# mLSTM chunks between the projection pairs, and two heads in turns in a recurrence's tile

## The chip, the cores and the metric

The program runs on one core of a Trainium2 chip. Its time is the device time of one launch, in microseconds (us). The kernel before takes 2728.09 us, the median of 3 runs (2724.17 to 2729.37).

A core has five engines that run their own instruction lists in order and wait for each other by semaphores: TensorE (PE, matmuls; PEld is its weight loads), VectorE (DVE), ScalarE (ACT), GpSimd (POOL) and SyncE (SP), which here issues all DMA transfers. Matmuls write to PSUM, which has eight banks; everything else lies in SBUF or in device memory.

## What is computed

One decoder layer of width 1024 on 2048 tokens in float32, and a final norm. The normalised input goes through one wide projection (`w_in`, 1024 to 10256 columns). Its columns feed four branches of width 512, and 4 x 1024 gates:

```python
h = rmsnorm(x, norm_g)
u = h @ w_in                         # split into the inputs of the branches and "merge"
y_a = rg_lru(causal_conv(lru_x)) * silu(lru_z)
hm  = mlstm_chunkwise(q, k, v, log_i, log_f)      # 4 heads of 128
y_b = (head_layernorm(sigmoid(m_o) * hm) + m_skip * xm) * silu(m_z)
y_c = head_rmsnorm(gla_chunkwise(hq, hk, h_i, log_fh)) * silu(h_z)     # 4 heads, key width 128
y_d = head_rmsnorm(gla_chunkwise(g_q, g_k, g_v, log_gk)) * silu(g_z)   # 4 heads, key width 64
merged = sum_n sigmoid(merge_n) * (y_n @ w_branch_n)
out = rmsnorm(x + merged @ w_out, final_g)
```

The mLSTM carries a 128 x 129 state per head from chunk to chunk, with stabilised exponentials. `gla_chunkwise` is a gated linear recurrence: within a chunk a lower triangular matrix of decayed query-key products times the values, plus the query times the carried state.

## The kernel before, in words

The 2048 tokens are done in two halves of 1024, and each half runs through the same stages. A float32 projection is split in two parts (`hi` and `lo`, rounded by ScalarE and subtracted by GpSimd) and done in three matmuls.

1. *Pairs* (`ahead_pairs`, 50 to 740 us in the first half, 1405 to 2085 us in the second). `ip_pair` projects two 128-column tiles for all 1024 tokens with seven products of twelve matmuls (L423), a block scheme that trades an eighth product for additions on VectorE (L428 on weights, L432 on results). The table `GORD` lists which pairs come in which order: `g` for the gates of the merge, `z` for the inputs of the branches, which are kept in device memory, `r` for the RG-LRU (done at once, with its matmuls L743), `d` for a decay, `m` for a step of the mLSTM's gate rows (`mlstm_rows`, L787 and L826), `t` for the change to the exponential and logarithm tables. Products go to the eight PSUM banks in turn (`bank8`).
2. *Mixers* (`mixers`, 740 to 1185 us and 2085 to 2545 us). Twelve tiles of the recurrences (`gla_tile`, 512 tokens each): eight of one head with key width 128 (HGRN2), then four of two heads with key width 64 (GLA), whose keys lie in partitions 0 to 63 and 64 to 127. A tile builds the triangular matrix from the diagonal outwards (L993, then L1036 for the blocks off the diagonal), transposes the keys (L1058), adds to the state (L1064), and forms the outputs: L1079 (matrix times values) and L1080 (query times state), which add up in one bank per head. Between the tiles the values are projected (`ip_vals`, L280) and some gates (L268). The mLSTM (`mlstm`, eight chunks of 128 tokens per half) runs beside them as a second generator: `both` advances it by 0.65 steps (`RATE`) for each step of a tile, after a start of eight steps (`LEAD`). Its matmuls are L863, L872, L879, L888, L900, L908, L909, L919 and L941, four or eight at a time.
3. *Merge* (`merge`): 32 products of a branch with `w_branch` (L268), each multiplied by its gate; its first products run already beside the last tiles of the mixers. Then the output projection (`outp`, L280).

The instructions are written in this order with priorities (`prio`), and a list scheduler places them: each engine's list is fixed when the program is built, by the durations that the scheduler assumes. On the chip an engine does not leave that order. TensorE's list therefore has, between the matmuls of a recurrence, a number of projection matmuls that was chosen to cover the wait.

Temporary tiles come from an arena of 16 slots (`NU`, of 516 columns), and of more slots in the mixers. In the pairs, slots 0 to 9 (`NG`) hold results of pairs and the others temporaries.

Of the kernel before, what the change touches and what calls it, by code (L numbers as in the profile page):

```python
# [21 lines left out]
NU = 16  # L22
# [4 lines left out]
EPS = 1e-6  # L27
NPB = 2
# [7 lines left out]
NW = 6  # L36
DG = (0,1)
NT = 16
# [3 lines left out]
GORD = [('g',2),('r',1),('z',1),('g',1),('z',1),('r',1),('g',1),('z',2),('r',1),('g',1),('z',2),('r',1),('z',6),('g',3),('t',0),('m',0),('g',1),('m',0),('g',1),('m',0),('g',1),('m',0),('d',0),('m',0),('g',99),('d',1),('z',2)]  # L42
# [105 lines left out]
class Trunk:  # L148
    def __init__(self, ctx, tc, a, out, dbg=None):
# [8 lines left out]
        self.wr = [c.tile([P, 528], F32, name=f"wr{k}") for k in range(3)]  # L158
# [9 lines left out]
        self.mi = 0  # L168
        self.ydram = [self.dram.tile([4, P, HT], F32, name=f"y{n}") for n in range(4)]
# [29 lines left out]

    def pbank(self):  # L200
# [38 lines left out]
    def wpieces(self, aps):  # L239
        nc = self.nc  # L240
        r = []
        with self.prio(self.EV):
            for ap in aps:
                w = ap.shape[-1]
                i = self.wi
                self.wi += 1
                raw, hi, lo = self.wr[i % 3][:, :w], self.wh[i % NW][:, :w], self.wl[i % NW][:, :w]
# [46 lines left out]
    def ip_tok_k(self, pieces, evac, ks):  # L294

        vs = [p[:, 0:256].unsqueeze(1) for p in [self.pbank() for _ in range(NPB)] + [self.bank() for _ in range(8 - NPB)]]
# [99 lines left out]
    def bank8(self):  # L396
        self.gi += 1
        return (self.pb + self.mx)[self.gi % 8]

    def ip_pair(self, t0, t1, fin, first=False):  # L400
# [5 lines left out]
        with self.prio(self.EV):  # L406
            b11, b12, b22 = (r[:, :512] for r in self.wr)
# [56 lines left out]
    def ahead_pairs(self):  # L464
# [72 lines left out]
        rows = (i for h in range(2) for i in self.mlstm_rows(h, temp))  # L537
        first = True
        for n, i in GORD:
# [5 lines left out]
            if n in "tm":  # L545
                continue
# [5 lines left out]
        assert not g and not z and not r and next(rows, 1)  # L552
# [278 lines left out]
    def mlstm(self):  # L831
# [10 lines left out]
        def load(n, c):  # L842
            t = self.T()
            nc.sync.dma_start(h4(t), self.pdram[n][:, :, c * 128:(c + 1) * 128].rearrange("h p t -> p h t"))
            return t

        def loads(c):
            g, cc = divmod(c, 4)
            r = []
            for i in range(2):  # L850
                t = self.T()
# [4 lines left out]
        def scores(c, xm, mx, r1b, wib):  # L856
# [7 lines left out]
            q, qw = self.T(), wib  # L864
# [3 lines left out]
            va = self.T()  # L868
# [20 lines left out]
            xs = self.T()  # L889
# [4 lines left out]
        def rest(c, xm, E, qw, va, xs, mo, z):  # L894
# [7 lines left out]
            hm = self.T()  # L902
# [21 lines left out]
            self.free(E, qw, va, xs)  # L924
            yield
# [23 lines left out]
        ld = loads(0)  # L949
        nxt = yield from scores(0, *ld)  # L950
        for c in range(8):
            cur = nxt
            mz = [load("mo", c), load("mz", c)]
            if c < 7:
                nxt = yield from scores(c + 1, *loads(c + 1))
            yield from rest(c, *cur, *mz)


    def gla_tile(self, n, gi, js, q, k, g, vs, zgs, heads, S, eps):
# [44 lines left out]
        for m in (8, 16, 32, 64):  # L1004
# [24 lines left out]
            else:  # L1029
                for h, (p0, K) in enumerate(heads):  # L1030
                    ps = self.bank()
                    for c in range(4):
                        for b in range(64 // m):
                            s0 = b * 2 * m
                            o = c * 128 + s0
                            T.matmul(ps[s0:s0 + m, c * m:(c + 1) * m], w[p0:p0 + K, o:o + m],  # L1036
                                     w[p0:p0 + K, o + m:o + 2 * m], start=True, stop=True)
                    for b in range(64 // m):
# [149 lines left out]
    def mixers(self):  # L1188
# [5 lines left out]
        other = self.mlstm()  # L1194
        due = 0.0

        def both(gen):

            nonlocal due
            for _ in iter(lambda: next(gen, 1), 1):  # L1200
                due += RATE
                while due >= 1:
                    due -= 1
                    next(other, None)

        with mix():
            for _ in range(LEAD):
                next(other, None)
# [15 lines left out]
        for s, (j, gi) in enumerate(steps):  # L1224
# [15 lines left out]
            with mix():  # L1240
                if j < 4:
                    both(self.gla_tile(2, gi, [j], *x, [hv[j][gi]], zs, [(0, 128)], self.S[j], self.eps_h))
                else:
                    p = j - 4
                    both(self.gla_tile(3, gi, [2 * p, 2 * p + 1], *x, gd[p][gi], [v[gi] for v in gv[2 * p:2 * p + 2]], zs,
                                       [(0, 64), (64, 64)], self.S[j], self.eps_g))
        with mix():
            for _ in other:
                pass
# [299 lines left out]
```

## Time and profile before

| | us |
|---|---|
| median of 3 runs | 2728.09 |
| profiled execution, its own time | 2737.6 |
| its span, first to last instruction | 2735.8 |
| TensorE busy | 2604.2 |
| VectorE busy | 1739.0 |
| GpSimd busy | 1500.4 |
| ScalarE busy | 1296.8 |

The busy time of TensorE is modelled from pipelined matmuls, so consecutive matmuls overlap in it: what one costs is read from the distance of two starts, and the busy time tells only where TensorE stood still. The granted clock is the mean of two levels, 1.2 and 2.4 GHz, as a share of the higher. A wait is put down to the releaser that came last.

### The profile page before, as it was taken

To read this page: it belongs to the slowest core of one execution; us is meant where nothing else is said; L and a number is where in the kernel's file an instruction comes from. 1 tells how busy PE (TensorE), PEld (TensorE's weight loads), DVE (VectorE), ACT (ScalarE), POOL (GpSimd) and SP (SyncE) were. 2 spreads that over 40 slices of the span, in tenths; PEclk is the share of its full clock that TensorE was granted. 3 is DMA by queue.
4 is the path that set the end of the run, shared out by engine and by line. 5 is a ranking of instruction groups with operands and counts; after the bars stand their busy time and mean duration, and the time that the engine had idled before them with its cause. 6 is when DMAs were issued, how large, how long until landed. Compare 5 with 4: busy or idle time off the path is not lost. (4 is left out here: it accounts for less than half of the span.)

```text
span 2735.8 us, 45795 instructions
## 1 busy us (share of the span) xinstructions
PE 2604.2 (95%) x16800; PEld 2155.0 (79%) x16800; DVE 1739.0 (64%) x2907; ACT 1296.8 (47%) x2769; POOL 1500.4 (55%) x1273
## 2 busy tenths in 40 slices
PE   7999999999998898999999999999999999999999
PEld 5777878878788886778977777788787888776789
DVE  8787676447667778634376957754657667775332
ACT  5455444434444464452454454454345455644533
POOL 5566556444555555466475566554445555654753
PEclk9999999999999998999999999999999989999999
DMA  6233223443454336785442432243346433558721
GB/s 227 70 127 104 85 85 131 135 135 112 156 178 126 103 123 205 271 288 160 140 139 77 140 115 85 89 131 124 123 131 203 129 106 120 183 168 289 260 95 74
DMA packets 227073, 393.03 MB, mean 144 GB/s; under 512 B 20721, under 2 KB 78081, under 8 KB 226849
## 3 DMA queue, kind: packets, MB, share of 16 engines
q1 hardware_dynamic: 226848, 390.11, 43.2%
q8 instruction: 132, 2.16, 0.3%
q14 instruction: 93, 0.75, 0.1%
HBM read 270.42 MB, written 119.60 MB: 143 GB/s over the span
## 5 line engine op out<-in xcount | busy, mean ns | idle before, releaser
L418 POOL TENSOR_TENSOR wl<-wr,wh 128x512 fp32r<-128x512 f32 x264 | 370.2, 1407 | 300.5 <-ACT wh L417 292.2
L418 POOL TENSOR_TENSOR wl<-gth,wh 128x512 fp32r<-128x512 f32 x198 | 286.4, 1447 | 280.7 <-ACT wh L417 266.7
L423 PE MATMUL mx<-s,wh 128*128 128x512 f32 x1248 | 395.0, 396 | 5.5 <-DVE arena L432 2.4
L432 DVE TENSOR_TENSOR arena<-arena,mx 128x512 f32<-128x512 f32 x386 | 252.8, 681 | 184.4 <-PE mx L423 168.1
L250 POOL TENSOR_TENSOR wl<-wr,wh 128x512 fp32r<-128x512 f32 (+1 forms) x176 | 248.5, 1420 | 194.1 <-ACT wh L249 159.3
L423 PE MATMUL mx<-hh,wl 128*128 128x512 f32 x824 | 328.1, 398 | 9.4 <-POOL wl L418 9.4
L423 PE MATMUL mx<-hh,wh 128*128 128x512 f32 x824 | 326.8, 397 | 5.8 <-DVE mqk L624 3.6
L423 PE MATMUL mx<-hl,wh 128*128 128x512 f32 x824 | 327.5, 397 | 2.4 <-DVE hl L306 2.3
L268 PE MATMUL pb<-hh,wh 128*128 128x512 f32 x704 | 291.0, 415 | 11.4 <-DVE lw L1319 4.0
L268 PE MATMUL pb<-hl,wh 128*128 128x512 f32 x704 | 287.6, 409 | 3.2 <-DVE hl L1293 3.2
L268 PE MATMUL pb<-hh,wl 128*128 128x512 f32 x704 | 286.5, 407 | 0.0
L423 PEld LDWEIGHTS mx<-s,wh 128*128 128x128 f32 x1248 | 235.7, 189 | 62.7 <-DVE arena L432 2.8
L417 ACT ACTIVATE wh<-wr 128x512 fp32r<-128x512 f32 x264 | 164.2, 627 | 229.0 <-PE mx L423 142.6
L280 PE MATMUL pb<-wh,hh 128*128 128x256 f32 (+1 forms) x880 | 254.2, 290 | 3.6 <-DVE lrt L1125 2.3
L280 PE MATMUL pb<-wl,hh 128*128 128x256 f32 (+1 forms) x880 | 253.9, 289 | 1.7 <-POOL wl L250 1.7
L280 PE MATMUL pb<-wh,hl 128*128 128x256 f32 (+1 forms) x880 | 253.5, 288 | 0.0
L423 PE MATMUL mx<-s,wl 128*128 128x512 f32 x624 | 245.5, 397 | 0.0
L417 ACT ACTIVATE wh<-gth 128x512 fp32r<-128x512 f32 x198 | 124.3, 628 | 228.5 <-DVE gth L428 184.4
L423 PEld LDWEIGHTS mx<-hh,wl 128*128 128x128 f32 x824 | 155.8, 189 | 51.5 <-POOL wl L418 16.0
L423 PEld LDWEIGHTS mx<-hh,wh 128*128 128x128 f32 x824 | 156.4, 190 | 46.3 <-issue 7.0
L249 ACT ACTIVATE wh<-wr 128x512 fp32r<-128x512 f32 (+1 forms) x176 | 110.2, 629 | 165.0 <-PE pb L268 110.1
L423 PEld LDWEIGHTS mx<-hl,wh 128*128 128x128 f32 x824 | 155.9, 189 | 41.1 <-DVE hl L306 3.6
(614 smaller groups left out, 6081.8 us busy)
## 6 DMA issues: line engine op xcount, KB each, us to landing
wr<-in_wc_dram SPq DMA_DIRECT2D x246, 256.0 KB, 2.7
g<-arena SPq DMA_DIRECT2D x52, 512.0 KB, 3.4
gth<-in_wc_dram SPq DMA_DIRECT2D x66, 256.0 KB, 2.8
wr<-in_wb_dram SPq DMA_DIRECT2D x64, 256.0 KB, 3.3
hl<-y SPq DMA_DIRECT2D x32, 512.0 KB, 5.9
arena<-g SPq DMA_DIRECT2D x48, 256.0 KB, 4.5
arena<-in_xT_dram SPq DMA_DIRECT2D x32, 256.0 KB, 5.2
lw<-g SPq DMA_DIRECT2D x32, 256.0 KB, 3.6
```

The source lines that it names most:

```text
L249: nc.scalar.activation(hi, raw, AF.Copy)
L250: nc.gpsimd.tensor_tensor(lo, raw, hi, op=ALU.subtract)
L268: nc.tensor.matmul(ps, w[:, ws], h[:, ts], start=(k == 0 and i == 0), stop=(k == nk - 1 and i == 2))
L280: self.nc.tensor.matmul(v, h[:, cs], w[:, ws], start=(first and i == 0), stop=(last and i == 2))
L417: A.activation(hi, w, AF.Copy)
L418: G.tensor_tensor(lo, w, hi, op=ALU.subtract)
L423: nc.tensor.matmul(ps, wp[:, ws], xp, start=(k == 0 and i == 0), stop=(k == 3 and i == 2))
L432: V.tensor_tensor(o, x, y, op=ALU.add)
```

## The change

- `mlstm` is a list of steps that `GORD` now calls with `c`, from the later pairs on: 53 steps per half, between eleven pairs. It takes its temporaries from the pairs' part of the arena (`temp`), loads the gate `mz` later, and starts a chunk before the one ahead of it is finished. `RATE`, `LEAD` and `both` are gone, and the mixers hold only the recurrences.
- While `c` steps are placed, the pairs' products use five PSUM banks (`fast`) and the mLSTM the other three (`slow`).
- In a tile of two heads, the blocks off the diagonal and both parts of the outputs alternate between the heads, each with a bank of its own. In all tiles the outputs are done as four (or eight) L1100 first, then four (or eight) L1104; only the first of a bank sets `start`.
- The change of tables (`t`) comes three pairs of gates earlier; the six gates per half of those pairs get their tanh in the merge (`NT` from 16 to 10).
- The arena has 22 slots for 16, the raw weights four buffers for three (`NR`); a scratch area of DMA is cut to 1024 bytes.

```diff
-NU = 16
+NU = 22
-RATE = 0.65
-LEAD = 8
+NR = 4
-NT = 16
+NT = 10
-GORD = [...,('z',6),('g',3),('t',0),('m',0),('g',1),('m',0),...,('d',0),('m',0),('g',99),('d',1),('z',2)]
+GORD = [...,('z',6),('t',0),('m',0),('g',1),('m',0),('g',1),('m',0),('c',2),('g',1),('m',0),('c',4),('d',0),('m',0),('c',4),('g',1),('c',5),...,('z',1),('c',4),('z',1),('c',4)]
...
+        self.fast, self.slow = self.pb + self.mx, self.mx
...
     def bank(self):
         self.mi += 1
-        return self.mx[self.mi % (8 - NPB)]
+        return self.slow[self.mi % len(self.slow)]
...
     def bank8(self):
         self.gi += 1
-        return (self.pb + self.mx)[self.gi % 8]
+        return self.fast[self.gi % len(self.fast)]
...
+        chunks = self.mlstm(temp)
...
+            elif n == "c":
+                self.fast, self.slow = self.pb + self.mx[:NF], self.mx[NF:]
+                with self.prio(RLAT):
+                    for _ in range(i):
+                        next(chunks)
...
-        ld = loads(0)
-        nxt = yield from scores(0, *ld)
+        last = None
         for c in range(8):
-            cur = nxt
-            mz = [load("mo", c), load("mz", c)]
-            if c < 7:
-                nxt = yield from scores(c + 1, *loads(c + 1))
-            yield from rest(c, *cur, *mz)
+            first = scores(c, *loads(c))
+            next(first)
+            yield
+            if last:
+                yield from last
+            cur = yield from first
+            last = rest(c, *cur, load("mo", c))
+            next(last)
+            yield
+            next(last)
+            yield
+        yield from last
...
-                for h, (p0, K) in enumerate(heads):
-                    ps = self.bank()
-                    for c in range(4):
-                        for b in range(64 // m):
-                            s0 = b * 2 * m
-                            o = c * 128 + s0
+                pss = [self.bank() for _ in heads]
+                for c in range(4):
+                    for b in range(64 // m):
+                        s0 = b * 2 * m
+                        o = c * 128 + s0
+                        for (p0, K), ps in zip(heads, pss):
                             T.matmul(ps[s0:s0 + m, c * m:(c + 1) * m], w[p0:p0 + K, o:o + m],
                                      w[p0:p0 + K, o + m:o + 2 * m], start=True, stop=True)
...
-        for h, ((p0, K), v, po) in enumerate(zip(heads, vs, pos)):
-            for c in range(4):
-                cc = slice(c * 128, (c + 1) * 128)
-                T.matmul(po[:, cc], atv[:, h, c], v[:, cc], start=True, stop=False)
-                T.matmul(po[:, cc], eg[p0:p0 + K, cc], sts[c][p0:p0 + K, :], start=False, stop=True)
+        for c in range(4):
+            cc = slice(c * 128, (c + 1) * 128)
+            for h, (v, po) in enumerate(zip(vs, pos)):
+                T.matmul(po[:, cc], atv[:, h, c], v[:, cc], start=(c == 0), stop=True, skip_group_check=c > 0)
+        for c in range(4):
+            cc = slice(c * 128, (c + 1) * 128)
+            for (p0, K), po in zip(heads, pos):
+                T.matmul(po[:, cc], eg[p0:p0 + K, cc], sts[c][p0:p0 + K, :], start=False, stop=True, skip_group_check=True)
```

How TensorE's list changes is seen at two places. The lists name a tile with its number (`mx_102` is a PSUM bank), the operands, and the size of the output; x4 are four in a row.

The outputs of a tile of two heads in the mixers of the first half, before. `mx_102` is the bank of the first head, `mx_103` that of the second.

```order
L1079 MATMUL mx_102<-mb_0_5086,arena 128x128
L1080 MATMUL mx_102<-arena,ma_0_5079 128x128
L1079 MATMUL mx_102<-mb_0_5086,arena 128x128
L1079 MATMUL mx_103<-mb_2_5088,arena 128x128
L1080 MATMUL mx_103<-arena,ma_0_5079 128x128
```

The two parts take turns, and the heads hardly do. Behind it, the outputs of such a tile after the change; here `mx_101` and `mx_102` are the banks of the two heads, L1084 adds to another tile's state, and L1012 is a diagonal block.

```order
L1100 MATMUL mx_101<-ma_3_5783,arena 128x128 x4
L1084 MATMUL mx_100<-ma_3_5783,arena 64x128
L1084 MATMUL mx_100<-arena 64x128
...
L1100 MATMUL mx_102<-arena 128x128 x4
L1104 MATMUL mx_101<-arena 128x128
L1104 MATMUL mx_102<-arena 128x128
L1012 MATMUL mx_105<-arena 32x32 x9
```

All L1100 stand together now, and the L1104 that follow alternate between the banks of the two heads.

The first groups of the mLSTM before, right after the pairs of the first half, among the projection of the values (L280).

```order
L280 MATMUL pb_97<-wh_85,hh_67 128x256
L280 MATMUL pb_97<-wl_91,hh_67 128x256
L280 MATMUL pb_97<-wh_85,hl_75 128x256
L888 MATMUL mx_99<-cst,ma_3_5082 128x128 x4
L872 MATMUL mx_103<-mwv,ma_3_5082 128x128 x4
L280 MATMUL pb_97<-wh_85,hh_68 128x256
```

After the change a chunk's groups stand between products of the pairs (L428). Here are three such groups: L891 (scores, bank `mx_104`), L954 (the last transposes of the chunk ahead, `mx_103`) and L900 (`mx_105`).

```order
L428 MATMUL pb_99<-s_8_588,wh_84 128x512 x2
L428 MATMUL pb_99<-s_8_588,wl_90 128x512
L891 MATMUL mx_104<-arena 128x128 x3
L954 MATMUL mx_103<-cst,arena 128x128 x4
L891 MATMUL mx_104<-arena 128x128
L900 MATMUL mx_105<-cst,arena 128x128 x4
L428 MATMUL pb_99<-s_9_589,wh_84 128x512 x2
L428 MATMUL pb_99<-s_9_589,wl_90 128x512
```

They moved from the mixers into the pairs, with about twenty matmuls of a pair between one such place and the next. The number of matmuls is the same in both programs. Of the merge's L268, 315 stand behind the last L1102 of the mixers before, and 444 behind its successor L1126 after.

## Rows read from the trace of the kernel before

**Rows 1.** The page: its first line, busy time by engine, one group of instructions.
```profile
span 2735.8 us, 45795 instructions
PE 2604.2 (95%) x16800; PEld 2155.0 (79%) x16800; DVE 1739.0 (64%) x2907; ACT 1296.8 (47%) x2769; POOL 1500.4 (55%) x1273
...
L417 ACT ACTIVATE wh<-wr 128x512 fp32r<-128x512 f32 x264 | 164.2, 627 | 229.0 <-PE mx L423 142.6
```

**Rows 2.** Busy time by stretch; the first row names the columns.
```profile
core 0: us, PE busy (x) PEld busy (x) DVE busy (x) ACT busy (x) POOL busy (x), PEclk, DMA share, GB/s
100.00:375.00 275.00, 267.27 (x1139) 214.43 (x1138) 193.23 (x246) 130.69 (x209) 157.51 (x112) 0.99 0.31 105
400.00:740.00 340.00, 340.00 (x1460) 268.38 (x1459) 204.77 (x288) 157.66 (x258) 167.70 (x127) 1.00 0.39 129
740.00:1185.00 445.00, 404.93 (x4226) 347.03 (x4224) 311.87 (x684) 217.44 (x625) 232.78 (x245) 0.96 0.54 174
1010.00:1185.00 175.00, 162.66 (x1734) 126.48 (x1732) 121.94 (x222) 81.26 (x216) 86.53 (x89) 0.94 0.67 230
2085.00:2545.00 460.00, 424.89 (x4276) 363.26 (x4276) 313.53 (x687) 229.18 (x653) 240.73 (x252) 0.94 0.55 177
```

**Rows 3.** TensorE's waits: total us, times, longest; two of each half's mixers.
```profile
PE mx L888 <- DMA ma<-pxm: 6.5, 1, 6.5
PE mx L908 <- DVE mb L884: 0.3, 1, 0.3
...
PE mx L863 <- DMA ma<-pxm: 8.1, 3, 4.5
PE mx L863 <- DMA mb<-pxm: 0.2, 1, 0.2
```

**Rows 4.** TensorE's timeline (start, duration, what, count, idle before), and two stretches there.
```profile
755.60 1.09 PE L888 MATMUL mx<-cst,ma 128*128 128x128 f32 x4 [6.54 <-DMA ma<-pxm]
...
2105.36 2.08 PE L863 MATMUL mx<-ma,mqk 128*128 128x128 f32 x8 [4.47 <-DMA ma<-pxm]
...
748.00:762.00 14.00, 7.46 (x45) 7.16 (x45) 11.12 (x22) 6.55 (x12) 6.31 (x5) 0.76 0.89 267
2100.00:2112.00 12.00, 7.53 (x52) 7.32 (x50) 8.61 (x19) 3.82 (x7) 5.83 (x5) 0.86 0.85 249
```

**Rows 5.** TensorE's timeline, two groups of an mLSTM chunk.
```profile
764.78 1.06 PE L879 MATMUL mx<-mb,ma 128*128 128x128 f32 x8
765.67 0.83 PE L872 MATMUL mx<-mwv,mb 128*128 128x128 f32 x6
```

**Rows 6.** TensorE's timeline in tiles of two heads.
```profile
1088.76 1.60 PE L1036 MATMUL mx<-ma 64*64 64x64 f32 x16
...
1097.68 1.09 PE L1064 MATMUL mx<-mb,arena 128*64 128x128 f32 x16
1098.70 0.49 PE L1079 MATMUL mx<-mb,arena 128*128 128x128 f32 x2
1099.12 0.48 PE L1080 MATMUL mx<-arena,ma 64*128 64x128 f32 x2
1099.54 0.71 PE L1079 MATMUL mx<-mb,arena 128*128 128x128 f32 x4
...
1105.21 0.49 PE L1080 MATMUL mx<-arena,ma 64*128 64x128 f32 x4
1105.63 0.49 PE L1079 MATMUL mx<-mb,arena 128*128 128x128 f32 x2
```

**Rows 7.** VectorE's groups, 740 to 1040 us: count, busy us, mean ns, idle before.
```profile
L922 DVE SCALAR_TENSOR_TENSOR Cst<-Cst,mdec,mx 128x129 f32<-128x129 f32 x32 | 9.6, 339 | 0.0
...
L937 DVE TENSOR_SCALAR mb<-mb,mmu,mvar 128x128 f32<-128x128 f32 x20 | 9.1, 513 | 3.2 <-ACT mvar L934 3.1
...
L943 DVE SCALAR_TENSOR_TENSOR ma<-mx,pvt,ma 128x128 f32<-128x128 f32 x16 | 4.5, 339 | 0.5 <-PE mx L941 0.5
L882 DVE SCALAR_TENSOR_TENSOR arena<-arena,mcols,cst 128x128 f32<-128x128 f32 x12 | 4.4, 425 | 4.3 <-DMA arena<-rdram 4.3
```

More of the change, by code (lines that the diff above doesn't have):

```diff
@@ L27 @@
 EPS = 1e-6
+NF = 3
 NPB = 2
@@ L157, in __init__ @@
         self.hl = [c.tile([P, HT], F32R, name=f"hl{k}") for k in range(KT)]
-        self.wr = [c.tile([P, 528], F32, name=f"wr{k}") for k in range(3)]
+        self.wr = [c.tile([P, 528], F32, name=f"wr{k}") for k in range(NR)]
         self.wh = [c.tile([P, 528], F32R, name=f"wh{k}") for k in range(NW)]
@@ L198, in free, with run @@
         self.ar.free(*aps)
+    def run(self, steps):
+        for _ in steps:
+            pass
     def pbank(self):
@@ L294, in ip_tok_k @@
     def ip_tok_k(self, pieces, evac, ks):
-        vs = [p[:, 0:256].unsqueeze(1) for p in [self.pbank() for _ in range(NPB)] + [self.bank() for _ in range(8 - NPB)]]
+        vs = [p[:, 0:256].unsqueeze(1) for p in [self.pbank() for _ in range(NPB)] + [self.bank() for _ in self.mx]]
         for k in ks:
@@ L406, in ip_pair @@
         with self.prio(self.EV):
-            b11, b12, b22 = (r[:, :512] for r in self.wr)
+            b11, b12, b22 = (r[:, :512] for r in self.wr[:3])
             b21, w2 = self.gth
@@ L551, in ahead_pairs @@
                 del {"g": g, "z": z, "r": r}[n][:i]
-        assert not g and not z and not r and next(rows, 1)
+        assert not g and not z and not r and next(rows, 1) and next(chunks, 1)
+        self.fast, self.slow = self.pb + self.mx, self.mx
     def setup(self):
@@ L892, in scores, with rest @@
             return xm, E, qw, va, xs
-        def rest(c, xm, E, qw, va, xs, mo, z):
+        def rest(c, xm, E, qw, va, xs, mo):
             emc = self.mcols[c // 4][:, c % 4, 2]
@@ L901, in rest @@
             so = mo
-            hm = self.T()
+            hm = temp()
             A.activation(hm[:, :512], po, AF.Copy)
@@ L924, in rest @@
             self.free(E, qw, va, xs)
+            z = load("mz", c)
             yield
@@ L1029, in gla_tile @@
             else:
-                for h, (p0, K) in enumerate(heads):
-                    ps = self.bank()
-                    for c in range(4):
-                        for b in range(64 // m):
-                            s0 = b * 2 * m
-                            o = c * 128 + s0
+                pss = [self.bank() for _ in heads]
[4 more added lines that the diff above has]
+                        for (p0, K), ps in zip(heads, pss):
                             T.matmul(ps[s0:s0 + m, c * m:(c + 1) * m], w[p0:p0 + K, o:o + m],
                                      w[p0:p0 + K, o + m:o + 2 * m], start=True, stop=True)
+                for h, ps in enumerate(pss):
                     for b in range(64 // m):
@@ L1193, in mixers @@
         self.gates_ahead(next(fill))
[L1194 to L1208, printed above, removed]
         hv = self.ip_vals(0, 256)
@@ L1241, in mixers @@
                 if j < 4:
-                    both(self.gla_tile(2, gi, [j], *x, [hv[j][gi]], zs, [(0, 128)], self.S[j], self.eps_h))
+                    self.run(self.gla_tile(2, gi, [j], *x, [hv[j][gi]], zs, [(0, 128)], self.S[j], self.eps_h))
                 else:
                     p = j - 4
-                    both(self.gla_tile(3, gi, [2 * p, 2 * p + 1], *x, gd[p][gi], [v[gi] for v in gv[2 * p:2 * p + 2]], zs,
+                    self.run(self.gla_tile(3, gi, [2 * p, 2 * p + 1], *x, gd[p][gi], [v[gi] for v in gv[2 * p:2 * p + 2]], zs,
                                        [(0, 64), (64, 64)], self.S[j], self.eps_g))
-        with mix():
-            for _ in other:
-                pass
         self.ar.base, self.ar.lim = 0, None
```

20 lines of the change are left out of this document (10 added, 10 removed).

## The prediction

> **What bounds the kernel now.** I read the page first, then the busy time by stretch, then who TensorE waits for, then its timeline. The page [rows 1] says that TensorE is busy for 2604 of 2736 us and every other engine for 64% or less: the time is TensorE's list of matmuls plus what it loses, so an edit counts only if it shortens that list or changes the losses. The stretches [rows 2] say where the losses are. In the second part of the pairs (400 to 740 us) TensorE stands still for nothing: 1460 matmuls in 340.00 us, 0.233 us each, at full clock. In the mixers it is idle for 445.00 - 404.93 = 40.1 us in the first half and 460.00 - 424.89 = 35.1 us in the second, and the clock averages 0.96 and 0.94, below which lie stretches at the lower level. The two mixers stages are 905 us of the span and hold 75 of its some 130 us of idle TensorE. The table of waits [rows 3] parts this idle time. In the first half nine rows, from 6.5 down to 0.3 us, are waits of mLSTM matmuls (L863, L872, L879, L888, L900, L908), together 20.2 us; in the second half six rows, from 8.1 to 0.2 us, 11.2 us. What remains, 19.9 and 23.9 us, are waits of the recurrences' tiles and of the projections between them. The two longest waits stand right at the start of the mixers, where the mLSTM's first loads have not landed: 6.54 and 4.47 us [rows 4].
>
> **The change, part by part.** The sum is made against the profiled execution, 2737.6 us (span 2735.8), which lies 9.5 us or 0.35% above the median of the runs.
>
> *The mLSTM's matmuls move.* Eight chunks of 60 instructions per half: a group of eight begins 0.89 us before the next group (765.67 - 764.78), 0.112 us each [rows 5]. 480 x 0.112 = 53.8 us per half leave the mixers, and the same 53.8 us join the pairs, whose TensorE had no gap to hide them in [rows 2]. Net: nothing. In the same way 444 - 315 = 129 matmuls of the merge that ran beside the last tiles now run behind them; 129 x 0.233 = 30 us per half change place and cost the same.
>
> *The waits at the start of the mixers go.* The first matmuls after the pairs are now 63 of L285's projection and then a tile of a recurrence. The waits of 6.54 and 4.47 us [rows 4] make 11.0 us. With them go two stretches of the lower clock: the mean of 0.76 over 14 us and 0.86 over 12 us [rows 4] means 6.7 and 3.4 us at half speed, a loss of half of that, 5 us. Together -16 us. At best all 31.4 us of mLSTM waits go, and 14 us of clock with them in the proportion of the start (31.4 x 5 / 11), -45 us; at worst none, if the first load of a chunk inside the pairs is as late.
>
> *The other mLSTM waits go with their matmuls.* 31.4 - 11.0 = 20.4 us stay in the sum, since a group still waits for VectorE or a load wherever it stands. What I add for the pairs: VectorE. Per chunk it has four each of L922, L937, L882 and L943 [rows 7], (339 + 513 + 425 + 339) x 4 = 6.5 us, and three 512-wide operations and a dozen narrow ones, estimated at 3 us from those means: some 75 us per half. The chunks stand among about 880 of the half's 2772 pair matmuls, 205 us, plus their own 54. VectorE's 205 of 340 us [rows 2] would give 124 us of the 205; with 75 it is 199 of 259, 77%. The nearest row is the first part of the pairs with the RG-LRU: VectorE 193 of 275 us, 70%, and TensorE idle for 275.00 - 267.27 = 7.7 us [rows 2]. In the same proportion two stretches of 259 us would cost 15 us; I take half, +7, because a product has five banks or 5 x 12 x 0.233 = 14 us before VectorE must have emptied one. Bounds: 0, and +31 if every wait of rows 3 comes twice. What queues behind a late chunk on VectorE are the additions (L432 before) of the pair, and on SP the next weights behind a store of the chunk's result.
>
> *The outputs of tiles with two heads.* Before, a pair of L1079 takes 1099.12 - 1098.70 = 0.42 us and the pair of L1080 after it 0.42 us [rows 6], so 0.84 us for a head and chunk, though four L1079 in a row take 0.64 us: the switch between the 128-row and the 64-row form costs about 0.1 us each way, and the first of a form stands alone. 8 tiles x 8 of these are 53 us; as some heads already meet, 48 us. After: 16 L1100 at 0.112 us and a switch, 2.0 us. For L1104 two rows tell what alternating heads do: four L1080 of two heads took 1105.63 - 1105.21 = 0.42 us, as long as two of one head, and 16 L1064, which alternate between the heads by column halves, took 1.02 us, 0.064 each. So 16 L1104 take 1.0 us at best, 1.7 us at 0.105 each, and 0.2 us for a switch. 3.2 to 3.9 us per tile, 26 to 31 us in all: 17 to 27 us less. I take -20 us. The two heads write separate banks (`mx_101`, `mx_102` in the list). The Trainium skill, TensorEngine Tiling (Array Packing), Restrictions and Gotchas, says that row tiles cannot work on one PSUM bank at the same time. That speaks against the alternation if a bank were shared; with L1104 at 0.112 us apiece this part would be -15 us. The trace shows the overlap for L1080, 0.42 us for four.
>
> *The blocks off the diagonal.* 16 L1036 of 64 x 64, two heads one after the other, took 1.5 us at the lower clock [rows 6], 0.77 us at full. Alternating, at most half goes, 0.4 us per tile; with the narrower blocks -4 us in all, at least 0. I take -2.
>
> *The mixers without cover.* With 54 us of mLSTM, 30 us of merge and some 11 us of outputs gone, TensorE's list in the mixers shrinks by 95 us per half, while VectorE loses 75 of 312 us. Its share goes from 70% to 237 of 350, 68%; GpSimd, with some 20 us of mLSTM work gone, from 52% to 61%. No engine becomes the bound, but a tile's chain has less time from one matmul group to the next. The 44 us of waits that are not the mLSTM's stay, and I add a quarter, +10 us. Bounds: -10, because VectorE's queue is shorter, and +44, when they double.
>
> *The rest.* Six gates' tanh per half are 12 activations of 512 columns, at 0.627 us [rows 1] 8 us, moved to the end of the mixers, where ScalarE is busy for 81 of 175 us [rows 2]: hidden, and 8 us at most where it is not. More arena slots and one more weight buffer (`NR`) let loads start earlier and cost nothing; no transfer here waits for the scratch area.
>
> Sum: -16 - 20 - 2 + 7 + 10 = -21 us, so 2716.6 for the profiled execution and 2728.09 x 2716.6 / 2737.6 = 2707 us for the median.
>
> **Rivals.** *Larger gain (2668 us).* The mLSTM's waits do not come back in the pairs, where about twenty matmuls or 4.6 us lie before each group, and the mixers gain from the freed VectorE: -27 - 45 - 4 - 10 = -86 us at the most; seven tenths of that, -60, give 2668. For it: 0.00 us idle between 400 and 740. Against it: VectorE at 77%.
>
> *The gain is swallowed (2728 us).* In the last four tiles TensorE gets done earlier and then waits for the tile's chain: VectorE has 122 us in 175 there [rows 2], GpSimd 87. If the tiles keep their pace, the outputs' 20 us turn into idle time, and the waits grow by a few more: 0. Against it: TensorE is busy for 163 of the 175 us.
>
> *Slower (2758 us).* Each chunk stalls the saturated pairs. A chunk is a chain over all engines; its groups stand at fixed places in TensorE's list, and a wait there stops the products too. At 4.5 us per chunk, the longest load wait of rows 3, 16 chunks cost 72 us for the 27 that I counted (20 + 7), so +45 on -21 gives +24, and with 6 us for the lower clock that follows some of them [rows 4] +30. It decides from (27 + 21) / 16 = 3.0 us per chunk. For it: VectorE's queue is long, and SP's transfers stand in line behind stores. Against it: in the mixers, under the same load, all chunks but the first ones cost 20 us for both halves.
>
> **How the numbers follow.** The forecast (2690 to 2722) has a chance of 0.50, the larger gain 0.16, the swallowed gain 0.14, the slower one 0.20. What a measurement of this kernel can tell from no change is about 0.2%, 5.5 us. Faster by more: the forecast, the larger gain and a little of the swallowed one, 0.68. Within: 0.12. Slower: 0.20. The range, 2662 to 2744, goes down to the larger gain and up to half way from no change to the slower case; it leaves out about one in ten on either side.
>
> **What would show it.** In the trace after: matmuls of the mLSTM lines among the pairs with waits of 27 us or less in all; a tile's 16 L1100 in 2.0 us and its 16 L1104 in 1.0 to 1.7 us; the mixers, from the last pair to the last L1126, near 350 us; idle TensorE there of 50 to 55 us for both halves. Waits of 3 us per chunk in the pairs, or idle time above 75 us in the mixers, would make the forecast wrong; L1104 at 0.112 us each would make the outputs' term too large.

## The result and the profile after

The changed kernel takes 2798.3 us against 2728.7 us for the kernel before: a ratio of 1.0253, interval 1.0229 to 1.0277, 70 us slower. 2707 us was forecast.

The page of the kernel after (span, busy time, TensorE's clock in 40 slices):

```profile
span 2790.8 us, 45738 instructions
PE 2601.2 (93%) x16800; PEld 2154.8 (77%) x16800; DVE 1787.2 (64%) x2907; ACT 1301.7 (47%) x2771; POOL 1506.4 (54%) x1273
PEclk9999999999999998999999999999999998999999
```

TensorE is busy for 2601 us, as before [rows 1], in a span that is 55 us longer (not 70: the profiled execution of the kernel before took 9 us more than its median, that of the kernel after 6 us less). A stretch of the pairs with chunks that answers to [rows 2], then both halves' mixers, from the last pair to the last matmul of a tile:

```profile
400.00:740.00 340.00, 326.39 (x1527) 263.24 (x1527) 234.77 (x388) 164.49 (x323) 164.90 (x127) 0.98 0.43 138
826.00:1200.00 374.00, 323.82 (x3636) 273.84 (x3634) 238.67 (x438) 187.26 (x480) 201.54 (x209) 0.91 0.44 147
2206.00:2572.00 366.00, 318.05 (x3636) 269.96 (x3634) 242.49 (x438) 181.89 (x478) 200.20 (x209) 0.93 0.44 150
```

The mixers of the kernel before, cut in the same way:

```profile
747.00:1199.00 452.00, 408.80 (x4243) 349.14 (x4242) 309.83 (x683) 228.82 (x660) 233.80 (x245) 0.96 0.55 179
2099.00:2552.00 453.00, 417.30 (x4244) 356.27 (x4243) 306.18 (x680) 230.51 (x660) 236.32 (x245) 0.94 0.55 177
```

The pairs, saturated before, lose 13.6 us in this stretch. The mixers last 374 and 366 us, where 350 was forecast. TensorE stands still in them for 50.2 and 47.9 us, 98 together, where it was 43.2 and 35.7, 79 together, although the mLSTM's waits are no longer in them. Their mean clock fell to 0.91 and 0.93 from 0.96 and 0.94. Where the mLSTM's first loads kept TensorE waiting for 6.54 and 4.47 us [rows 4], a recurrence's tile now does:

```profile
838.10 0.66 PE L1012 MATMUL mx<-mb 128*32 128x32 f32 x32 [3.85 <-DVE mb L1035]
2219.77 0.65 PE L1012 MATMUL mx<-mb 128*32 128x32 f32 x32 [5.44 <-DVE mb L1035]
```

What TensorE waits for in the first half's pairs (total, times, longest; the four largest). L838 transposes the gate rows, which waited for nothing in the pairs before. The other three are matmuls of chunks, and [rows 3] had their like in the mixers:

```profile
PE mx L838 <- ACT arena L832: 4.4, 1, 4.4
PE mx L884 <- DMA arena<-pmx: 3.0, 2, 1.9
PE mx L875 <- DMA arena<-pxm: 1.5, 1, 1.5
PE mx L931 <- DVE arena L926: 1.2, 1, 1.2
```

The outputs of a tile with two heads [rows 6], now by turns, and all 64-row products of this kind by shape, of the kernel after and (next fence) before:

```profile
1092.31 0.38 PE L1100 MATMUL mx<-ma,arena 128*128 128x128 f32 x2
1093.65 0.49 PE L1100 MATMUL mx<-mb,arena 128*128 128x128 f32 x2
...
1095.40 0.49 PE L1104 MATMUL mx<-arena 64*128 64x128 f32 x4
1097.19 0.94 PE L1104 MATMUL mx<-arena 64*128 64x128 f32 x12
1098.06 0.50 PE L273 MATMUL pb<-hl,wh 128*128 128x512 f32 x1
L1104 PE MATMUL mx<-arena 64*128 64x128 f32 x128 | 12.2, 300 | 0.9 <-DVE arena L1091 0.9
```

```profile
L1080 PE MATMUL mx<-arena 64*128 64x128 f32 x96 | 19.9, 323 | 0.0
L1080 PE MATMUL mx<-arena,ma 64*128 64x128 f32 x32 | 6.8, 322 | 0.0
```

128 of them took 26.7 us of busy time and take 12.2. Two things changed for them at once: they stand together, and the heads take turns. In the mixers of the kernel after, one stall shows the chain that the experiments then followed (start, duration, [idle before <- releaser]):

```profile
930.26 0.69 DVE L1127 TENSOR_TENSOR arena<-mx,arena 128x512 f32<-128x512 f32 x1 [5.08 <-PE mx L1126]
930.97 0.32 SPq L1130 DMA_DIRECT2D y<-arena  x1
933.04 1.23 DVE L987 TENSOR_TENSOR_SCAN arena<-cst,mb 128x512 f32<-128x512 f32 x1 [2.10 <-DMA y<-arena]
934.35 0.61 POOL L1031 TENSOR_TENSOR arena<-arena 128x256 f32<-128x256 f32 x1 [12.14 <-DVE arena L987]
934.30 0.63 ACT L1069 ACTIVATE ma<-arena 128x512 f32<-128x512 f32 x1 [12.16 <-DVE arena L987]
938.39 0.66 PE L1012 MATMUL mx<-arena 128*32 128x32 f32 x32 [8.05 <-DVE arena L1035]
```

L1130 stores one tile's result; L987 is the scan that opens the next. It is given the slot that the store still reads, so it waits 2.10 us for the transfer, and before that for all that the store itself waited for (L1126, L1127). GpSimd and ScalarE stand for 12 us meanwhile, and TensorE for 8.05. Over the whole run, what the opening scans waited for (first line) and the two largest groups of those that waited for them:

```profile
  DMA y<-arena: 13.4, 4
  POOL arena L1031: 35.3, 6
  ACT ma L1069: 29.7, 4
```

### The profile page after: what moved, and what is told of

Read it like the earlier page. It is cut to its first block, busy times and chain, and to the rows that moved or that the text cites. A ratio compares the mean times of both kernels' runs of the same rounds, so it can differ in the third digit from the quotient of the medians.

```text
span 2790.8 us, 45738 instructions
## 1 busy us (share of the span) xinstructions
PE 2601.2 (93%) x16800; PEld 2154.8 (77%) x16800; DVE 1787.2 (64%) x2907; ACT 1301.7 (47%) x2771; POOL 1506.4 (54%) x1273
## 4 chain that ended last, share of the span: by engine, by line
PE 69%; DVE 10%; DMA 5%; POOL 4%; issue 4%; ACT 3%; SPq 0%; POOLq 0%; DVEq 0%; ACTq 0%
PE mx L428 28%; PE pb L273 13%; PE pb L428 11%; PE pb L285 7%; POOL wl L423 1%; PE mx L285 1%; PE mx L1100 1%; PE mx L1012 1%; PE mx L1104 1%; DMA ob<-in_x_dram 1%; DMA y<-arena 1%; PE mx L1055 1%; PE mx L1126 1%; PE mx L1084 1%; DVE arena L1035 1%
## 5 line engine op out<-in xcount | busy, mean ns | idle before, releaser
L428 PE MATMUL mx<-s,wh 128*128 128x512 f32 x1104 | 353.0, 399 | 8.8 <-DVE s L311 4.3
L428 PE MATMUL mx<-hh,wh 128*128 128x512 f32 x776 | 310.2, 400 | 11.4 <-DVE mcols L840 4.0
L428 PE MATMUL mx<-hh,wl 128*128 128x512 f32 x776 | 310.2, 400 | 6.3 <-POOL wl L423 6.3
L428 PE MATMUL mx<-hl,wh 128*128 128x512 f32 x776 | 310.1, 400 | 3.2 <-DVE hl L311 3.2
L273 PE MATMUL pb<-hh,wh 128*128 128x512 f32 x704 | 290.0, 414 | 16.3 <-DVE gth L1325 5.4
L437 DVE TENSOR_TENSOR arena<-arena,mx 128x512 f32<-128x512 f32 x346 | 227.2, 679 | 116.4 <-PE mx L428 100.4
L428 PEld LDWEIGHTS mx<-s,wh 128*128 128x128 f32 x1104 | 208.2, 189 | 60.1 <-DVE s L311 7.3
L428 PE MATMUL mx<-s,wl 128*128 128x512 f32 x552 | 217.1, 397 | 0.0
L428 PEld LDWEIGHTS mx<-hh,wh 128*128 128x128 f32 x776 | 148.1, 191 | 47.1 <-ACT wh L422 4.6
L285 PEld LDWEIGHTS pb<-wh,hh 128*128 128x128 f32 x880 | 171.0, 195 | 16.6 <-DVE arena L1147 9.9
L428 PEld LDWEIGHTS mx<-hh,wl 128*128 128x128 f32 x776 | 147.6, 190 | 44.1 <-POOL wl L423 10.9
```

The costliest lines, as they stand in the source:

```text
L273: nc.tensor.matmul(ps, w[:, ws], h[:, ts], start=(k == 0 and i == 0), stop=(k == nk - 1 and i == 2))
L285: self.nc.tensor.matmul(v, h[:, cs], w[:, ws], start=(first and i == 0), stop=(last and i == 2))
L428: nc.tensor.matmul(ps, wp[:, ws], xp, start=(k == 0 and i == 0), stop=(k == 3 and i == 2))
L437: V.tensor_tensor(o, x, y, op=ALU.add)
```

## The experiments

Times are medians; "before" ran beside each (2728.5 to 2730.6 us), so a difference between runs of different batches carries some 2 us from that alone.

**The change in pieces.** *turns_alone*: the kernel before with the new gla_tile alone. *move_alone*: the kernel after with the old gla_tile. *params*: the kernel before with these alone:

```diff
-NU = 16
+NU = 22
+NR = 4
-NT = 16
+NT = 10
-GORD = [...('z',6),('g',3),('t',0),('m',0)...]
+GORD = [...('z',6),('t',0),('m',0)...]
-    nc = bacc.Bacc("TRN2", target_bir_lowering=False, num_devices=1)
+    nc = bacc.Bacc("TRN2", target_bir_lowering=False, num_devices=1, dynamic_dma_scratch_size=1024)
```

> The kernel before with nothing changed but the recurrence tile: the two heads of a gla tile take turns in the off-diagonal products and the outputs. Theory A (the mixers run dry once the chunks are gone, the turns themselves are a gain): the outputs cost TensorE 39.5 us in a half before and 28.2 us after, so about 11 us in each half go and some of it returns as waits: 2703 to 2715 us. Rival D (the turns do harm, for instance because both heads' banks are held together and a product waits for the slower head): 2728 us or more.

2724.6 us, ratio 0.9989 (0.9970 to 1.0007): no difference that can be told.

> The kernel after with the recurrence tile as it was before: the chunks run between the pairs, the heads do not take turns. Theory A: all of the loss is in the move, and the turns give back some 10 us a half: 2810 to 2822 us. If the mixers are bound by the tile's own chain of VectorE, ScalarE and GpSimd, the turns are hidden there and this run stays at 2798 us. Rival D: below 2790 us.

2820.3 us, 22.0 above the kernel after: what theory A said of the turns. Its other part, that all of the loss is in the move, falls with the next run.

> The kernel before with only the side parameters of the change: 22 slots in the memory pool instead of 16, four raw weight buffers instead of three, ten gates with their tanh ahead instead of sixteen and the turn of the activation tables three gate pairs earlier, the smaller DMA scratch. The chunks stay in the mixers and the heads do not take turns. Theory C (some of the 70 us comes from these, as the 6 us longer start and the 10 to 20 us longer last part of each half suggest): 2740 to 2755 us. Theories A and B: 2724 to 2733 us.

2788.9 us, ratio 1.0223 (1.0190 to 1.0255). Theory C, and larger than it said. Before to params +60, params to move_alone +31, move_alone to after -22: that is the 70. By stage (us; pairs from the first to the last matmul of ip_pair, mixers from there to the last of gla_tile, rest to the next pairs or the end):

| | first pair at | pairs | mixers | rest | pairs | mixers | rest |
|---|---|---|---|---|---|---|---|
| before | 53.7 | 693.2 | 452.4 | 216.7 | 682.8 | 453.2 | 183.9 |
| params | 59.1 | 692.9 | 475.9 | 224.3 | 677.9 | 468.9 | 188.5 |
| move_alone | 59.4 | 764.6 | 385.3 | 254.8 | 748.0 | 386.8 | 217.4 |
| after | 59.8 | 766.6 | 373.4 | 256.1 | 750.6 | 365.4 | 219.0 |

The parameters cost 39 us in the mixers, where they name nothing. The mixers of params:

```profile
752.00:1228.00 476.00, 426.02 (x4223) 360.94 (x4222) 314.99 (x678) 240.41 (x676) 237.43 (x243) 0.91 0.49 162
2130.00:2599.00 469.00, 419.46 (x4224) 355.89 (x4223) 316.20 (x677) 244.43 (x679) 236.60 (x246) 0.92 0.52 169
```

With the chunks still in them, they hold 50.0 + 49.5 = 99.5 us of idle TensorE and a clock of 0.91 and 0.92, much as the kernel after does: both come with the parameters alone. The move adds 71.7 and 70.1 us to the pairs, 17.9 and 16.3 above its 53.8 of matmuls.

**The parameters one by one**, each on the kernel before: `NU` with the scratch area (slots22), `NR` (raw4), `NT` with `GORD` (tables_early).

> The kernel before with 22 slots in the memory pool instead of 16, and the smaller DMA scratch that makes room for them; nothing else. The run with all side parameters took 60 us more than before, 39 of them in the two mixers stages, 5 at the start and 12 after the mixers. Theory C1 (more slots turn the rotation of the pool, so that tiles in the mixers are given the slots that the tile just before them still reads, and run one after the other; the start and the rest are not touched): 2760 to 2772 us, with the mixers of 476 and 469 us again. Rival C2 (the fourth raw buffer or the earlier turn of the tables does it, by other transfers or a fuller ScalarE in the mixers): 2725 to 2735 us.

2762.2 us, +32: ratio 1.0119 (1.0103 to 1.0135). That is C1's time, but the mixers took 468 and 456 us, not 476 and 469.

> The kernel before with four raw weight buffers instead of three; nothing else. Theory C1: the mixers stay near 452 us each; the 5 us at the start may be this (weights are fetched earlier, in front of the input's tiles), 2728 to 2735 us. Rival C2: 2750 to 2765 us. Theory of the prediction (one more buffer costs nothing): 2728 us.

2749.9 us, +20: ratio 1.0075 (1.0059 to 1.0091), the first pair 8 us later and the rest of the first half 8.5 us longer, not the mixers: C1's place, at more than its price.

> The kernel before with ten gates' tanh ahead instead of sixteen and the turn of the activation tables three gate pairs earlier; nothing else. Six gates' tanh move to the merge, 12 activations of 0.63 us in each half, which is where params lost 7.6 and 4.6 us. Theory C1: 2732 to 2742 us, the loss behind the mixers. Rival C2: 2750 to 2765 us with the mixers longer. Theory of the prediction (hidden): 2728 us.

2739.8 us, +10: ratio 1.0039 (1.0019 to 1.0059). That is C1's time; where it is lost the traces can't show, since the profiled executions took nearly the same (2738.7 us here, 2737.6 before). The three make 62, as params did together.

**The slots.** A rotating pointer hands out slots; with 22 instead of 16 it comes round at another point. *old_slots* (on the kernel after) and *params_old* take, in the mixers (`self.old`), the slot that was freed longest ago (`freed` holds a count that `free` raises):

```diff
-        u = us[0]
+        u = min(us, key=lambda u: self.freed.get(u, 0)) if self.old and k == 1 else us[0]
```

> The kernel after with one change in the choice of memory slots: within the mixers a tile takes the free slot that was freed longest ago, not the next one in rotation. In the kernel after, the scan that opens a tile waits in some tiles for the store of the previous tile's result, because it is given the slot that this store still reads. Theory A1 (this reuse makes the tiles run one after the other, and without the chunks nothing covers it): the two gaps of 4.7 and 8.05 us before the products at 925 and 938 us and their like at the starts go in both halves, with the stretches at the low clock behind them: 2760 to 2775 us. Rival A2 (the mixers are bound by the work of the tile's chain, not by the slots): 2790 to 2798 us. Theory B (the loss is in the pairs): 2798 us.

2774.7 us, 24 less. The scans' waits of the kernel after have become:

```profile
  POOL mb L1071: 5.0, 2
  POOL arena L995: 1.2, 2
  POOL ma L1047: 0.7, 1
```

No store holds a scan up any more, and GpSimd and ScalarE wait for the scans for 50 us where it was 92. But the waits where the mixers begin stayed (3.07 and 4.59 us), against A1, and TensorE's idle time in the mixers fell only from 98 to 92.5 us: most of the 24 us is not located.

> The kernel with all side parameters of the change on top of the kernel before (2788.9 us), and in the mixers the slot that was freed longest ago in place of the next in rotation. Theory C1: the mixers come back from 476 and 469 us to 445 to 455 each, 2740 to 2755 us. Rival C2 (the slots are not it): 2785 to 2792 us.

2765.5 us, 23 less, between C1 and C2: the mixers won 30 and 26 us, as C1 had it, and 14 and 20 went back in the rest. The mixers hold 123 matmuls fewer, which now run behind them.

On slots22, with its counterpart where the mixers end:

```diff
         self.ahead = 0
+        self.ar.used[16:NU] = [True] * (NU - 16)
```

> The kernel of slots22 (the kernel before with 22 slots, 2762 us) with the six new slots set aside while the mixers run, so that the tiles there are given the very slots, in the same turn, that they had with 16; the pairs keep all 22. Theory C1 (what costs is only which slot the rotation hands to a tile): 2726 to 2735 us. Rival C3 (the smaller scratch area, or the pairs' use of the slots, costs it): 2755 to 2765 us.

2807.2 us: neither. ScalarE's timeline while the pairs still run, and its table loads of L227 from 740 to 1260 us:

```profile
677.59 1.28 ACT L1312 ACT_TABLE_LOAD   x1
678.89 0.63 ACT L1312 ACTIVATE arena<-arena 128x512 f32<-128x512 f32 x1
...
705.80 1.28 ACT L227 ACT_TABLE_LOAD   x1
707.09 1.16 ACT L227 ACTIVATE arena<-arena 128x512 f32<-128x512 f32 x2
708.27 1.28 ACT L1142 ACT_TABLE_LOAD   x1
...
L227 ACT ACT_TABLE_LOAD x27 | 34.6, 1283 | 0.5
```

Three tanh of the merge in each half (L1312; the first one is shown) found free slots and ran while the table that serves exponential and logarithm together was in use. From there nearly each logarithm (L227: 27 loads for 28 activations in this window, 2 loads in the kernel before) and the exponentials behind it load a table of their own: 143 loads in the whole run, 183.5 us of ScalarE, where the kernel before has 35, 44.9 us. In slots22_hide2 the slots are given back only where the output projection begins, so that neither the mixers nor the merge get them.

> The kernel of slots22_hide, but with the six new slots set aside until the output projection begins, not only while the mixers run. In slots22_hide a gate's tanh of the merge (L1312) got one of the free slots and came into the mixers' list, and each exponential after it had to load its table again. With that gone, theory C1 (which slot the rotation hands out is what costs): 2726 to 2738 us, the mixers near 452 us each. Rival C3 (the smaller scratch area, or what the pairs do with 22 slots): 2752 to 2765 us.

2723.8 us, ratio 0.9982 (0.9968 to 0.9996): C3 falls, and the time is just below C1's range. The small scratch area and what the pairs do with more slots cost nothing; all 32 us come with the six slots being free to the mixers and the merge. That the turn of the rotation is what costs there, as C1 says, is not shown by it: the opening scans of slots22 wait 6.4 us for stores in all and those of slots22_hide2 1.2, and GpSimd and ScalarE wait for the scans for 30 and 27 us. The mixers of slots22 and (second fence) of slots22_hide2:

```profile
748.00:1217.00 469.00, 416.48 (x4247) 354.77 (x4246) 318.14 (x679) 236.91 (x668) 236.09 (x248) 0.94 0.52 170
2112.00:2569.00 457.00, 405.54 (x4222) 346.96 (x4221) 313.34 (x677) 236.51 (x665) 229.79 (x243) 0.94 0.52 172
```

```profile
744.00:1197.00 453.00, 416.07 (x4242) 353.80 (x4241) 309.87 (x683) 226.38 (x657) 233.05 (x245) 0.95 0.54 175
2090.00:2536.00 446.00, 411.73 (x4244) 351.71 (x4243) 310.77 (x682) 231.28 (x659) 229.74 (x244) 0.96 0.55 176
```

Nearly the same number of matmuls (x), and 52 us of idle TensorE in each half against 37 and 34.

**The raw buffer.** raw4_late goes through three buffers where raw4 lost time:

```diff
-                raw, ... = self.wr[i % NR][:, :w], ...
+                raw, ... = self.wr[i % self.nr][:, :w], ...
+        self.nr = NR  (mixers begin)
+        self.nr = 3   (start, output projection)
```

> The kernel of raw4 (the kernel before with four raw weight buffers, 2750 us) with the fourth used only in the mixers and the merge; at the program's start and in the output projection, where the next half's input is loaded too, three are in turn as before. Theory C4 (the fourth buffer lets a weight's transfer into SP's queue ahead of the input's tiles, and these come later: 8 us more at the start, 8.5 us between the halves): 2728 to 2735 us. Rival C5 (it costs in the mixers and the merge): 2744 to 2752 us.

2741.1 us (2730.5 to 2744.6): about half. Between 1300 and 1430 us, the output projection, raw4's two long waits (first fence) are down to 1.2 and 0.7 us in raw4_late (second), where L282 and L687 answer to L281 and L686:

```profile
PE pb L281 <- POOL wl L251: 4.9, 2, 4.3
PE mx L686 <- DVE rsx L673: 3.4, 1, 3.4
```

```profile
PE pb L282 <- POOL wl L252: 1.2, 1, 1.2
...
PE mx L687 <- DVE rsx L674: 0.7, 1, 0.7
```

The first pair still begins at 57.3 us (before 53.7, raw4 62.1). The fourth buffer costs in the projection, as C4 says; that the order of SP's transfers is the reason is not shown. The other 10 us stay open, and this trace can hold little of them: the profiled execution took 2733.4 us.

**The move.** The two edits of the kernel after (rows_first, chunks_calm):

```diff
-...('m',0),('c',2),('g',1),('m',0),('c',4),('d',0),('m',0),('c',4),('g',1)...
+...('m',0),('g',1),('m',0),('d',0),('m',0),('c',5),('g',1)...
```

```diff
-                with self.prio(RLAT):
+                with self.prio(0):
                     for _ in range(i):
                         next(chunks)
```

> The kernel after with the chunks' 48 steps begun only when the last step of the gates' rows has been issued, and spread over the nine places behind it (5 or 6 steps each); nothing else moved. In the kernel after the pairs hold about 12 us more idle TensorE in each half than with the same parameters and the chunks in the mixers, most of it between 621 and 648 us, where the rows' last transposes wait 4.4 us for ScalarE and the chunks' first loads 3 us, with 13.6 us at the low clock. Theory B1 (the chunks and the rows hold each other up there): this cluster goes, some 8 us of idle time and 5 us of clock in each half: 2770 to 2785 us. Rival B2 (every chunk costs some 2 us of waits wherever it stands): 2793 to 2803 us.

2791.5 us, a ratio of 1.0228 (1.0210 to 1.0246) to before, which overlaps that of the kernel after: between B1 and B2, and settles neither. (A half has 48 steps of chunks, not the 53 named under "The change".) Nor were the chunks only spread: 92 of the first half's 480 matmuls and 48 of the second's now run behind the pairs, in the mixers.

> The kernel after with the chunks' instructions given the priority of the place where they are written, not that of 2000 instructions earlier: TensorE gets them later than they are ready. Theory B1 or B2 (waits of chunk groups inside the pairs cost 34 us in both halves): with more time between a group and what feeds it the waits go, 2765 to 2785 us, if the chunks' ends do not run into the mixers. Rival (the waits are loads and ScalarE's queue, which come later as well): 2793 to 2803 us.

2796.9 us, in the rival's range. TensorE's waits from 400 to 830 us add up to 15.0 us, where they were 14.6 in the kernel after: that the chunks come later did not shorten them. The rival's reason is not shown; the largest wait is now L954's for VectorE, 5.9 us in all. Then the chunks' arithmetic (`scores`, `rest`) was replaced by a load and a store, on two kernels with the choice of old_slots: turns_old (below) and the kernel after with `NR = 3`:

> The kernel after with three raw weight buffers and the slot that was freed longest ago; 22 slots, the early tables, the moved chunks and the turns stay. If the costs of the side parameters add up in the kernel after as they did in the kernel before (raw buffer 20 us, slots 24 us in old_slots): 2798 - 20 - 24 = 2754 us. If the fourth buffer costs only where the chunks stand in the mixers: 2774 us.

2761.4 us, nearer to the first: 37 less.

> The kernel of turns_old (2712.7 us, chunks in the mixers) with the chunks' arithmetic left out: each of the eight chunks only loads one tile of the gates and stores it as the branch's result. 107.6 us of TensorE's matmuls go in both halves together. Theory T1 (in the mixers the chunks were the cover: they ran in gaps that the recurrences' tiles leave): the time falls by less than their matmuls, 65 to 90 us, to 2623 to 2648 us. Rival T2 (the chunks brought as many waits as they filled): it falls by 107 us or more, 2605 us or less.

2603.3 us, 109.4 less: T1 falls, T2 holds. Both mixers of no_chunks_mix and (second fence) of turns_old:

```profile
747.00:1095.00 348.00, 311.53 (x3593) 263.35 (x3592) 240.34 (x436) 176.69 (x474) 205.32 (x209) 0.92 0.47 160
2045.00:2392.00 347.00, 318.23 (x3666) 271.69 (x3664) 243.59 (x445) 180.80 (x479) 208.44 (x216) 0.95 0.53 177
```

```profile
747.00:1171.00 424.00, 387.31 (x4162) 333.39 (x4161) 302.44 (x679) 230.65 (x659) 226.64 (x238) 0.94 0.53 171
2089.00:2511.00 422.00, 387.15 (x4182) 333.68 (x4181) 304.48 (x679) 228.99 (x659) 223.89 (x238) 0.95 0.55 176
```

In the first half's mixers TensorE idles for 36.5 us without the chunks and for 36.7 with them, in the second half's for 28.8 and 34.9, and over the whole span for 128.5 and 126.0. In all they neither filled gaps nor made any: they cost about their 107.6 us of matmuls (960 x 0.112, by [rows 5]). The waits for the first loads, 5.0 and 5.6 us in turns_old, are gone; behind the same pairs the values' projection now waits 3.3 and 2.9 us for VectorE, and the first matmul of a tile behind it 1.9 and 2.1.

> The kernel of after_raw3_old (2761.4 us, chunks among the pairs, 22 slots, early tables) with the chunks' arithmetic left out in the same way. Theory B2 (among the pairs there is no gap to fill, and each chunk adds some 2 us of waits and low clock): the time falls by 107.6 + 30 = 138 us, to 2615 to 2632 us, close to what the kernel without chunks in the mixers takes and some 10 us for the tables. Theory of the prediction (+7 for the pairs): it falls by about 115 us, to 2646 us.

2632.1 us, 129.3 less: 21.7 more than the matmuls, 15.6 of them in the pairs' stages; nearer to B2, at the upper end of its range, than to the prediction's +7.

**A faster kernel.** The choice of old_slots on turns_alone and on the kernel before:

> A version meant to beat both: the kernel before with the heads' turns (2724.6 us alone) and, in the mixers, the slot that was freed longest ago; 16 slots, three raw buffers and the tables as before, the chunks in the mixers. Theory C1 (slots decide how far tiles overlap): on the side parameters of the change this choice gave 23 us, but with 16 slots only three tiles are given a slot of the tile just before, and the mixers hold 44 and 44 us of idle TensorE: 2700 to 2718 us. Rival (with the old rotation the slots are not what the mixers wait for, VectorE and ScalarE are): 2720 to 2728 us.

2712.7 us, ratio 0.9940 (0.9925 to 0.9955), in C1's range.

> The kernel before with nothing changed but the choice of slots in the mixers: the one freed longest ago. The turns alone gave 4 us on the kernel before, turns and this choice together 16 us. If each works for itself: 2714 to 2719 us. If the turns gain only where tiles may overlap (TensorE's shorter lists end in a wait for the next tile's slot otherwise), this choice alone is worth little: 2722 to 2729 us.

2706.9 us, ratio 0.9909 (0.9888 to 0.9931): below both ranges. The kernel before with the slot freed longest ago is the fastest that does all of the work, and the turns add nothing to it.

The same choice takes 24 us from 16 slots (2730.6 to 2706.9) and 23 from params with its 22 (2788.9 to 2765.5). So it does not undo what the 22 slots cost: params_old stays 59 us above before_old, and the raw buffer and the tables make 30 of these, if costs add up. Some 29 us stay with the 22 slots although no pointer decides in the mixers any more. What the six slots cost 32 us by is open; the order of the rotation alone is not it.

## Why the prediction was wrong

The forecast was -21 us and the change made +70. Piece by piece, the numbers of the change were forecast at 0 and cost 60, the move at -16 + 7 + 10 = +1 and cost 31, the turns at -22 and gave 22.0. The step that failed first is *The rest*: "More arena slots and one more weight buffer (`NR`) let loads start earlier and cost nothing", with the tanh "hidden". Measured: 32, 20 and 10 us. I counted what the numbers add and took them to change nothing else. But slots that are free to the mixers and the merge change what may start when and what waits for what: the 32 us go when the six slots are withheld there (slots22_hide2). One such wait is seen whole in the kernel after, a scan behind a store with TensorE standing for 8.05 us; which waits make up the 32 us is open.

*The waits at the start go* (-16) failed too. The chunks left out altogether gave 1.8 us beyond their matmuls, within what two batches differ by, where 16 were promised: TensorE's wait was only named after the matmul that stood first in the list. The tile behind it waits 3.85 and 5.44 us in its place in the kernel after, and a projection and a tile 5.2 and 5.0 in no_chunks_mix.

*The mLSTM's matmuls move at no cost*: right, 109.4 for 107.6 us. *The waits in the pairs*: 20.4 carried over and +7, together 27; measured 21.7 on one pair of kernels and 34 by stage on another. The size was near, but nothing was saved in the mixers to pay for it, so that all of it is loss where the sum had +7. That the size was near is in part luck. The +7 was scaled from 7.7 us of idle time beside a VectorE at 70%, and all of that idle time (100 to 375 us of the kernel before) ended with a weight's split by GpSimd or ScalarE, none with VectorE:

```profile
PE mx L423 <- POOL wl L418: 4.1, 4, 1.7
PE pb L423 <- ACT wh L417: 1.1, 1, 1.1
PE mx L423 <- ACT wh L417: 1.1, 1, 1.1
PE pb L423 <- POOL wl L418: 1.0, 1, 1.0
PE pb L743 <- POOL wl L733: 0.4, 1, 0.4
```

The slower rival's price, 4.5 us for each of 16 chunks (the longest load wait of [rows 3] is in fact 6.5), did not come: 1.4 to 2.1.

*The outputs* (-20) and *the blocks* (-2): 22.0 between move_alone and after, and the rows as forecast, 12 L1104 in 0.94 us. Yet the same edit gave 4 us on the kernel before, within the noise, and nothing on before_old (2706.9, and 2712.7 with it). The shorter list is certain; that it shortens the time is not, and that the sum's -22 was met to the tenth is in part luck.

*The mixers without cover* (+10): idle TensorE there is 98 us, above the 75 named as the sign of a wrong forecast. But missing cover was not the cause: params, with the chunks in place, has 99.5, and no_chunks_mix, without them, 65.2 where turns_old has 71.5.

Open: by what the six slots cost 32 us, what in raw4 still costs 10 us with raw4_late, where the tables' 10 go, and which waits of the chunks could be avoided among the pairs.

## What to carry to other kernels

A change of a pool's size or of a buffer count is a change of the order in which work may overlap: look, for each long chain, at which earlier reader its first write must wait for, and try giving out the slot freed longest ago where chains follow one another (here it took some 24 us off three kernels and 12 off a fourth). An idle time named after an instruction does not go when that instruction goes; ask what stands behind it and whether that would be ready. When an edit carries numbers along with its idea, price the numbers apart: here they were 60 of 70 us.

## What the runs showed of the hardware

A table load takes 1.283 us. Six tanh that came too early, three in each half, went with 108 more loads than in the kernel before, 138.6 us of ScalarE, and with 83 us of time (2723.8 to 2807.2). Two heads' 64-row products that stand together and go by turns, in banks of their own, ran in less than half the busy time (26.7 to 12.2 us for 128): twelve took 1098.06 - 1097.19 = 0.87 us, 0.073 each, where products of 128 rows took 0.112 [rows 5]. The Trainium skill, TensorEngine Tiling (Array Packing), Restrictions and Gotchas, says that row tiles cannot work on one PSUM bank at the same time; with a bank for each head the trace shows the overlap. No run put both heads in one bank.
